# Fourteen of the first FFN's 22 inner tiles by seven block products instead of eight, with weight sums made by adding DMAs

## The chip, the cores and the metric

The kernel runs on one core of one Trainium2 chip. The metric is the device time of one execution in microseconds (us); lower is better. TensorE multiplies, VectorE, ScalarE and GpSimd work on tiles of 128 partitions in SBUF and PSUM, and SyncE (SP) issues most of the DMAs. In rows of the profile PE is TensorE, PEld its weight load, DVE VectorE, ACT ScalarE and POOL GpSimd.

## What is computed

The reference is a trunk of two layers on 512 tokens of width 1024: a conformer convolution module and an FFN, then retention with four heads and a second FFN. The change is in the first FFN (`F` = 2816, 22 tiles of 128 columns):

```python
def conv_ffn(x, w_in, dw_w, dw_b, w_out):
    h = x @ w_in                       # x (512, 1024), w_in (1024, 2 * 2816)
    a, u = jnp.split(h, 2, axis=-1)
    a = causal_dwconv(a, dw_w, dw_b)   # three taps along the tokens, each column by itself
    return (jax.nn.silu(a) * u) @ w_out

for i in range(DEPTH):
    ...
    h = rmsnorm(x, norm_ffn_g[i])
    x = x + conv_ffn(h, ffn_w_in[i], ffn_dw_w[i], ffn_dw_b[i], ffn_w_out[i])
```

Retention turns q and k by angles `positions * inv_freq`; the tables of their cosine and sine (128 x 512 each) are made while the first FFN runs.

## The kernel before

**Three matmuls for one.** Every operand is split into a high part that TensorE reads at its fast precision (type fp32r) and the low remainder, and a product is high x high, high x low and low x high, added up in PSUM (`mm3`, L272 to L274). Weights come from DRAM in chunks of up to 1 MB (`wr`, 128 x 2048), in the order in which they are used (`_chunks`), on SP's DMA queue. ScalarE casts a half of a chunk (128 x 1024) to its high part `wh` (L229) and VectorE subtracts it for the low part `wl` (L233). A unit of weights is what one call of `weights()` hands to TensorE, and the emission runs up to two units ahead of it; there are four buffers each for `wh` and `wl`.

**One inner tile of the FFN** (`ffn_half`, L785 to L831). `mm(f)` makes `fa` and `fu`, 128 inner columns x 512 tokens each, in PSUM: 8 row blocks x 3 matmuls with 512 columns moving. The x that they read is split before it is normalised, so each result still lacks the factor 1/rms of its token (`norm.rb`, shown as `n1r`). `evac(f)` puts it in: VectorE multiplies `fa` by it into `ap` (L812), ScalarE and VectorE do the three taps and SiLU (`ft`, L814 to L817), GpSimd scales `ft` for `fu`'s sake (L818), VectorE multiplies `fu` by it (`fy`, L820), and `fy` is split (`yh`, `yl`; L348, L349). After 12 tiles the output projection `fo0` multiplies their y's by `w_out` and adds to x, and after the other 10 `fo1` does. `fo1`'s additions also build the square sums for the next norm, n2.

**The tables.** `rotary_tables` (L836 to L877) is a generator: after each tile from the third on, one step of four GpSimd instructions on 128 x 512 is put out (multiply, round, subtract, add: L863, L856, L857, L871).

**Seven products.** Retention's value and gate projections already multiply 2 x 2 blocks with seven products in the heads 1 to 3 (`ret_vg_blocks`, tiles `vg1z` to `vg3p`). The sums of weight blocks for them are made by VectorE (L255), those of x by `left_sums` (L922 to L929).

A scheduler orders the instructions of each engine by an estimate of the time line; each engine then runs its own queue in that order and waits on semaphores.

## Time and profile before

| | us |
|---|---|
| median of 3 runs | 1292.96 |
| lowest, highest | 1292.64, 1293.29 |
| the profiled execution | 1293.24 |
| its span in the trace | 1291.5 |
| first FFN in it, by the rows of its tiles | about 182 to 549 |

TensorE's granted clock is at its full level (1.00) throughout the first FFN. Read the page from the share of each engine and the chain that ended last to the stage at hand; the busy times of the stage, not those of the span, tell what is free there.

### The profile page before, as it was taken

To read this page: it belongs to the slowest core of one execution; us is meant where nothing else is said; L and a number is where in the kernel's file an instruction comes from. 1 tells how busy PE (TensorE), PEld (TensorE's weight loads), DVE (VectorE), ACT (ScalarE), POOL (GpSimd) and SP (SyncE) were. 2 spreads that over 40 slices of the span, in tenths; PEclk is the share of its full clock that TensorE was granted. 3 is DMA by queue.
4 is the path that set the end of the run, shared out by engine and by line. 5 is a ranking of instruction groups with operands and counts; after the bars stand their busy time and mean duration, and the time that the engine had idled before them with its cause. 6 is when DMAs were issued, how large, how long until landed. Compare 5 with 4: busy or idle time off the path is not lost.

```text
span 1291.5 us, 15110 instructions
## 1 busy us (share of the span) xinstructions
PE 1282.0 (99%) x5955; PEld 1067.0 (83%) x5955; DVE 810.0 (63%) x1036; ACT 520.9 (40%) x703; POOL 355.2 (28%) x305
## 2 busy tenths in 40 slices
PE   9999999999999999999999999999999999999997
PEld 7889988888888888888888888878888888888886
DVE  6998657665335554579696596596675643355542
ACT  6646644333124333334435335354443431233332
...
GB/s 330 225 123 106 148 98 70 127 66 130 98 98 66 130 49 114 131 81 106 106 42 160 138 14 180 103 83 116 97 76 145 94 143 98 98 66 131 33 65 65
DMA packets 35926, 140.48 MB, mean 109 GB/s; under 512 B 10896, under 2 KB 15760, under 8 KB 21776
## 3 DMA queue, kind: packets, MB, share of 16 engines
q1 hardware_dynamic: 32256, 134.02, 30.2%
q10 hardware_dynamic: 3600, 5.52, 1.5%
q8 instruction: 46, 0.75, 0.2%
...
## 4 chain that ended last, share of the span: by engine, by line
PE 96%; DVE 2%; issue 1%; ACT 0%; POOL 0%; POOLq 0%
PE fa L272 6%; PE fa L274 6%; PE fu L273 6%; PE fu L272 6%; PE fu L274 6%; PE fa L273 6%; PE lo L272 3%; PE fo L273 3%; PE fo L274 3%; PE lo L273 3%; PE lo L274 3%; PE fo L272 3%; PE cph L539 2%; PE ro L272 2%; PE ro L273 2%; PE ro L274 2%
## 5 line engine op out<-in xcount | busy, mean ns | idle before, releaser
L233 DVE TENSOR_TENSOR wl<-wr,wh 128x1024 fp32r<-128x1024 f32 (+2 forms) x242 | 302.7, 1254 | 207.2 <-ACT wh L229 203.7
L229 ACT CAST wh<-wr 128x1024 fp32r<-128x1024 f32 (+2 forms) x244 | 250.5, 1029 | 372.0 <-PE fo L274 82.7
L811 POOL MEMSET ap<- 128x2 f32 x44 | 4.2, 99 | 371.7 <-DVE ft L816 305.4
L988 POOL TENSOR_TENSOR gg<-gg,gn 128x512 f32<-128x512 f32 x16 | 27.5, 1719 | 179.3 <-ACT gg L987 179.3
L820 DVE TENSOR_TENSOR fy<-fu,ft 128x512 f32<-128x512 f32 x44 | 30.4, 690 | 68.6 <-PE fu L274 35.0
L814 ACT ACTIVATE ft<-ap,prm 128x512 f32<-128x512 f32 x44 | 35.8, 814 | 71.3 <-DVE ap L812 71.3
L588 DVE SCALAR_TENSOR_TENSOR tp<-hp,prm,tp 128x512 f32<-128x512 f32 x80 | 55.8, 747 | 0.4
L579 POOL TENSOR_TENSOR pla<-pla,plt 128x512 f32<-128x512 f32 x36 | 49.1, 1365 | 9.8 <-ACT pla L575 5.7
L815 DVE SCALAR_TENSOR_TENSOR ft<-ap,prm,ft 128x512 f32<-128x512 f32 x44 | 37.2, 844 | 17.7 <-ACT ft L814 17.5
L817 ACT ACTIVATE ft<-ft 128x512 f32<-128x512 f32 x44 | 27.9, 633 | 45.0 <-DVE ft L816 44.6
L972 POOL TENSOR_TENSOR rs<-rs 128x512 f32<-128x512 f32 x16 | 24.7, 1559 | 67.5 <-DVE rs L971 43.7
L818 POOL TENSOR_TENSOR ft<-ft,n3r 128x512 f32<-128x512 f32 x22 | 32.1, 1461 | 29.0 <-ACT ft L817 29.0
L818 POOL TENSOR_TENSOR ft<-ft,n1r 128x512 f32<-128x512 f32 x22 | 31.6, 1434 | 28.8 <-ACT ft L817 28.8
L816 DVE SCALAR_TENSOR_TENSOR ft<-ap,prm,ft 128x512 f32<-128x512 f32 x44 | 35.8, 814 | 1.5
L578 ACT ACTIVATE plt<-hp,prm 128x512 f32<-128x512 f32 x36 | 25.8, 722 | 20.6 <-POOL pla L579 20.2
L539 PEld LDWEIGHTS cph<-ph,cmat 128*128 128x128 f32 x288 | 32.6, 192 | 0.2
L539 PE MATMUL cph<-ph,cmat 128*128 128x128 f32 x288 | 32.6, 275 | 0.0
L430 DVE TENSOR_TENSOR xT<-ro,xT 128x512 f32<-128x512 f32 x32 | 21.6, 682 | 15.6 <-PE ro L274 15.6
L255 DVE TENSOR_TENSOR wr<-wr,wr 128x1024 f32<-128x1024 f32 x24 | 28.8, 1211 | 0.0
L812 DVE TENSOR_TENSOR ap<-fa,n3r 128x512 f32<-128x512 f32 x22 | 15.1, 690 | 20.5 <-PE fa L274 20.5
L812 DVE TENSOR_TENSOR ap<-fa,n1r 128x512 f32<-128x512 f32 x22 | 15.1, 689 | 17.2 <-PE fa L274 17.2
L856 POOL TENSOR_SCALAR near<-prod 128x512 f32<-128x512 f32 x11 | 22.9, 2085 | 0.9
...
## 6 DMA issues: line engine op xcount, KB each, us to landing
wr<-in_weights_dram SPq DMA_DIRECT2D x106, 1024.0 KB, 4.9
...
wr<-in_weights_dram SPq DMA_DIRECT2D x4, 512.0 KB, 3.4
...
```

What stands on the lines that cost most here:

```text
L229: latest[0] = act.copy(hi[:, o:o + n], raw[:, s + o:s + o + n])
L233: latest[1] = low_on.get(i, dve).tensor_tensor(out=lo[:, o:o + n], in0=raw[:, s + o:s + o + n], in1=hi[:, o:o + n].bitcast(F32), op=ALU.su ...
L272: pe.matmul(ps, wh, xh, start=first, stop=False, **check)
L273: pe.matmul(ps, wl, xh, start=False, stop=False, **check)
L274: pe.matmul(ps, wh, xl, start=False, stop=last, **check)
L539: pe.matmul(ps[:, g * P:(g + 1) * P], mats[i][g][:, s, :], ph[:, g, NSH - 1 - s:NSH - 1 - s + P], start=s == 0, stop=s == NSH - 1)
L579: gate[0] = pool.tensor_tensor(out=pl, in0=pl, in1=tm, op=ALU.add).ins
L588: dve.scalar_tensor_tensor(out=a, in0=hp[:, t:t + S], scalar=tap(t, i), in1=a, op0=ALU.mult, op1=ALU.add)
L814: act.activation(t, ap[:, 2:], AF.Identity, scale=wc(2), bias=wc(3))
L815: dve.scalar_tensor_tensor(out=t, in0=ap[:, 1:1 + S], scalar=wc(1), in1=t, op0=ALU.mult, op1=ALU.add)
L816: dve.scalar_tensor_tensor(out=t, in0=ap[:, 0:S], scalar=wc(0), in1=t, op0=ALU.mult, op1=ALU.add)
L818: scaled = pool.tensor_tensor(out=t, in0=t, in1=norm.rb, op=ALU.mult)
```

## The change

Columns 8 to 13 and 14 to 21 of the 22 inner tiles are now made in pairs, a pair being 256 columns of a and the 256 of u that belong to them. Take x as 2 x 2 blocks (token half by half of the 1024 rows) and the pair's weights as 2 x 2 blocks (row half; a in column 1, u in column 2). Seven block products give the pair where eight did. Each product has 2 inner tiles x 4 row blocks x 3 matmuls with 256 columns moving. The groups of inner tiles are now 0 to 7 (as before), 8 to 13 and 14 to 21, each with its output projection (`fo0`, `fo1`, `fo2`).

- *Weights.* A pair's weights are two chunks `wr`, one holding W11 and W12, the next W21 and W22. The seven factors in order of use are W11, W21, `ws`, then W11, W12, W21, W22 again after sums have been added to them in place. `ws` = W11 + W12 is one VectorE addition into a buffer of its own. W12 += W22 is a DMA from DRAM that adds to what lies in SBUF; it is issued with the loads, during the pair before. W11 += W12 is an adding DMA within SBUF, issued when factor 1 is handed out, W21 += W11 the same at factor 2. All three are issued by GpSimd. Each factor is then cast and subtracted like any unit.
- *Left operands.* `Factors` makes four sums of the normalised x, one step per tile of the first group, and the normalised x itself is split anew ahead of `fo0`. The results of the second and third group therefore need no scaling by 1/rms, and GpSimd's L818 falls away for them.
- *Evacuation* (`ffn_blocks`). Five of the seven products run in one bank per tile, `fz`; between them ScalarE copies intermediate results out (`q1`, `u1`, `u2`). `fx` and `fp` are two more. The three taps (`taps`) are as before; the memset goes to VectorE.
- *Tables.* The same arithmetic on VectorE, a step per tile of the second and third group. Six tiles borrow buffers of other names (`rot0` to `rot5`).
- The pool of the FFN's tiles has 8 buffers for y where it had 12.

Core of the diff:

```diff
-HALVES = [(0, 12), (12, 22)]
+GROUPS = [[(0, 8, False), (8, 14, True), (14, 22, True)], [(0, 12, False), (12, 22, False)]]
...
     def ffn(l):
-        for f0, f1 in HALVES:
+        for f0, f1, by_blocks in GROUPS[l]:
             for f in range(f0, f1, 2):
-                cols("ffn_w_in", l, 0, 8, (f * P, 256))
-                cols("ffn_w_in", l, 0, 8, (F + f * P, 256))
...
+    def prepare_pair(i):
+        for j in (i, i + 1):
+            next(load_weights(j))
+        w = raws[i, "sum"] = sum_pool[0].tile([P, 1024], F32, tag="ws", bufs=1, name=f"ws{i}")
+        dve.tensor_tensor(out=w, in0=raws[i][:, :1024], in1=raws[i][:, 1024:], op=ALU.add)
+        pool.dma_start(raws[i][:, 1024:], weights_d[i + 1, :, 1024:], accum_op=ALU.add)
+    def pair_factor(i, n):
+        for j in (i, i + 2) if n == 3 else (i,):
+            if j in pairs and j not in raws:
+                prepare_pair(j)
+        w11, w12, w = raws[i][:, :1024], raws[i][:, 1024:], raws[i, "sum"]
+        w21, w22 = raws[i + 1][:, :1024], raws[i + 1][:, 1024:]
+        if n == 1:
+            pool.dma_start(w11, w12, accum_op=ALU.add)
+        if n == 2:
+            pool.dma_start(w21, w11, accum_op=ALU.add)
+        return (w11, w21, w, w11, w12, w21, w22)[n]
...
+        def turns(dst, src):
+            dve.tensor_scalar(out=near, in0=src, scalar1=MAGIC, scalar2=-MAGIC, op0=ALU.add, op1=ALU.add)
+            return dve.tensor_tensor(out=dst, in0=src, in1=near, op=ALU.subtract)
...
+    class Factors:
+        def __init__(self, norm, xs, pool_, other):
+            self.norm, self.xs, self.other = norm, xs, other
+            self.sums = [pool_.tile([P, 4, 4, N2], F32R, tag=f"s{half}", bufs=1, name=f"{norm.name}s{half}") for half in "hl"]
...
+        def sums_of(self, k):
+            x1, x2 = self.normed(k), self.normed(k + 4)
+            lo, hi = slice(0, N2), slice(N2, S)
+            a = xp.tile([P, 2, N2], F32, tag="nacc", bufs=1, name=f"{self.norm.name}sa{k}")
+            b = self.other(f"{self.norm.name}sb{k}")
+            dve.tensor_tensor(out=a[:, 0], in0=x1[:, hi], in1=x2[:, hi], op=ALU.subtract)
+            dve.tensor_tensor(out=a[:, 1], in0=a[:, 0], in1=x1[:, lo], op=ALU.subtract)
+            dve.tensor_tensor(out=b[:, 0], in0=x1[:, lo], in1=x1[:, hi], op=ALU.subtract)
+            dve.tensor_tensor(out=b[:, 1], in0=x2[:, lo], in1=a[:, 1], op=ALU.add)
+            for o, t in ((0, a), (2, b)):
+                h, l = (u[:, k, o:o + 2, :] for u in self.sums)
+                act.copy(h, t)
+                dve.tensor_tensor(out=l, in0=t, in1=h.bitcast(F32), op=ALU.subtract)
+        def normed_split(self, k):
+            self.xs[k] = split(self.normed(k), f"{self.norm.name}n{k}", ("xh", "xl"), xp8)
...
+    def ffn_blocks(fp, l, norm, f0, f1, left, side=None):
+        ys = []
+        for f in range(f0, f1, 2):
+            def bank(which):
+                return [psum(f"f{which}{l}_{f + j}")[:, :N2] for j in range(2)]
+            def product(pss, which, first=False):
+                w = weights()
+                for j, ps in enumerate(pss):
+                    for k, (xh, xl) in enumerate(left.factor(which)):
+                        mm3(ps, *w(k, j * P, (j + 1) * P), xh, xl, first and k == 0, k == 3, skip_group_check=not first)
+            def kept(pss, name):
+                tiles = [fp.tile([P, N2], F32, tag=name, bufs=2, name=f"{name}{l}_{f + j}") for j in range(2)]
+                for t, ps in zip(tiles, pss):
+                    act.copy(t, ps)
+                return tiles
+            lo, hi = slice(0, N2), slice(N2, S)
+            aps = [fp.tile([P, S + 32], F32, tag="ap", bufs=2, name=f"ap{l}_{f + j}") for j in range(2)]
+            us = [fp.tile([P, S], F32, tag="fy", bufs=2, name=f"fy{l}_{f + j}") for j in range(2)]
+            z = bank("z")
+            product(z, "x11", True)
+            q1 = kept(z, "q1")
+            x = bank("x")
+            product(x, "x12", True)
+            for j in range(2):
+                dve.memset(aps[j][:, :2], 0.0)
+                dve.tensor_tensor(out=aps[j][:, 2:2 + N2], in0=x[j], in1=q1[j], op=ALU.add)
+            p = bank("p")
+            product(p, "s1", True)
+            product(z, "s2")
+            u1 = kept(z, "u1")
+            product(z, "s3")
+            u2 = kept(z, "u2")
+            for j in range(2):
+                dve.tensor_tensor(out=us[j][:, hi], in0=p[j], in1=u2[j], op=ALU.subtract)
+            product(z, "x22")
+            ts = []
+            for j in range(2):
+                act.copy(aps[j][:, 2 + N2:2 + S], z[j])
+                ts.append(taps(fp, l, f + j, aps[j]))
+            product(p, "s4")
+            for j in range(2):
+                dve.tensor_tensor(out=us[j][:, lo], in0=p[j], in1=u1[j], op=ALU.subtract)
+                dve.tensor_tensor(out=us[j], in0=us[j], in1=ts[j], op=ALU.mult)
+                ys.append(split(us[j], f"y{l}_{f + j}", ("yh", "yl"), fp))
+                next(side or iter(()), None)
+        return ys
...
+        left = Factors(n1, list(n1.xs), fp, lambda name: fp.tile([P, 2, N2], F32, tag="fy", bufs=2, name=name))
+        def sums_of_x():
+            yield
+            for k in range(4):
+                left.sums_of(k)
                 yield
-    with ExitStack() as es:
-        fp = es.enter_context(tc.tile_pool(name="f0", reuse_waits="tile", bufs=12))
-        rp = es.enter_context(tc.tile_pool(name="rot", reuse_waits="tile", bufs=1))
-        n2 = Norm(mix_g[1], "n2")
-        rot = rotary_tables(rp)
-        for n, (f0, f1) in enumerate(HALVES):
-            ys = ffn_half(fp, 0, n1, f0, f1, () if n else (None, n1.stats, n1.bcast), rot)
-            proj_out(ys, f"fo{n}", n2 if n else None)
-        for _ in rot:
-            pass
+        for n, (f0, f1, by_blocks) in enumerate(GROUPS[0]):
+            if by_blocks:
+                ys = ffn_blocks(fp, 0, n1, f0, f1, left, rot)
+            else:
+                ys = ffn_half(fp, 0, n1, f0, f1, (None, n1.stats, n1.bcast), each=sums_of_x())
+                for k in range(KD):
+                    left.normed_split(k)
+                rot = rotary_tables(fp)
+                next(rot)
+            n2 = Norm(mix_g[1], "n2") if f1 == NF else None
+            proj_out(ys, f"fo{n}", n2)
+        assert next(rot, None) is None
```

On ScalarE, around tiles 16 and 17, stood before (`ft` the taps, `wh` a chunk's high part, `y0_16h` the high part of y):

```order
L814 ACTIVATE ft0_16_3582<-ap0_16_3579,prm_95 128x512
L817 ACTIVATE ft0_16_3582<-ft0_16_3582 128x512
L348 CAST y0_16h_3590<-fy0_16_3588 128x512
L229 CAST wh36_0_3456<-wr36_3454 128x1024
L229 CAST wh36_1024_3460<-wr36_3454 128x1024
L814 ACTIVATE ft0_17_3667<-ap0_17_3664,prm_95 128x512
L229 CAST wh37_0_3596<-wr37_3594 128x1024
L817 ACTIVATE ft0_17_3667<-ft0_17_3667 128x512
L229 CAST wh37_1024_3600<-wr37_3594 128x1024
```

and stands now (`q10_16`, `u10_16` copies of `fz`; `wh59` to `wh63` the high parts of factor 3 to 6 of one pair and 0 of the next, from `wr36` = W11, W12 and `wr37` = W21, W22):

```order
L239 CAST wh59_0_4128<-wr36_3856 128x1024
L929 COPY q10_16_4080<-fz0_16_4049 128x256
L929 COPY q10_17_4081<-fz0_17_4050 128x256
L239 CAST wh60_0_4156<-wr36_3856 128x1024
L385 CAST y0_14h_4027<-fy0_14_3782 128x512
L973 ACTIVATE ft0_15_3992<-ft0_15_3992 128x512
L239 CAST wh61_0_4188<-wr37_3858 128x1024
L239 CAST wh62_0_4222<-wr37_3858 128x1024
L929 COPY u10_16_4184<-fz0_16_4049 128x256
L385 CAST y0_15h_4037<-fy0_15_3783 128x512
L929 COPY u10_17_4185<-fz0_17_4050 128x256
L239 CAST wh63_0_4262<-wr38_4121 128x1024
```

The casts of `wh59` to `wh61` read weights to which an adding DMA has written; the copies `u10_16` and `u10_17` now stand behind `wh61`, whose sum is the last of the three to be issued.

On GpSimd stood before, in the first half (here at tile 4), a table step and the scaling of each tile:

```order
L818 TENSOR_TENSOR ft0_4_2273<-ft0_4_2273,n1r_1923 128x512
L863 TENSOR_SCALAR prod_2130<-rc0_2122 128x512
L856 TENSOR_SCALAR near_2131<-prod_2130 128x512
L857 TENSOR_TENSOR prod_2130<-prod_2130,near_2131 128x512
L871 TENSOR_TENSOR turn_2129<-turn_2129,prod_2130 128x512
L811 MEMSET ap0_7_2519 128x2
```

and in the second and third group stand now only the adding DMAs, three to a pair (here those into `wr36`, `wr37` and into `wr38`, `wr39`):

```order
L282 DMA wr36_3856<-in_weights_dram 128x1024
L292 DMA wr36_3856<-wr36_3856 128x1024
L294 DMA wr37_3858<-wr36_3856 128x1024
L282 DMA wr38_4121<-in_weights_dram 128x1024
L292 DMA wr38_4121<-wr38_4121 128x1024
L294 DMA wr39_4123<-wr38_4121 128x1024
```

On VectorE stood before, for tile 17 (`ap` the evacuation, L815 and L816 the taps, `wl` low parts):

```order
L812 TENSOR_TENSOR ap0_17_3664<-fa0_17_3529,n1r_1923 128x512
L233 TENSOR_TENSOR wl36_1024_3461<-wr36_3454,wh36_1024_3460 128x1024
L815 SCALAR_TENSOR_TENSOR ft0_17_3667<-ap0_17_3664,prm_95,ft0_17_3667 128x512
L816 SCALAR_TENSOR_TENSOR ft0_17_3667<-ap0_17_3664,prm_95,ft0_17_3667 128x512
L233 TENSOR_TENSOR wl37_0_3597<-wr37_3594,wh37_0_3596 128x1024
L820 TENSOR_TENSOR fy0_17_3673<-fu0_17_3554,ft0_17_3667 128x512
L233 TENSOR_TENSOR wl37_1024_3601<-wr37_3594,wh37_1024_3600 128x1024
L349 TENSOR_TENSOR y0_17l_3676<-fy0_17_3673,y0_17h_3675 128x512
```

and stands now, where the pair of 14 and 15 ends and that of 16 and 17 runs (L503 and L490 are a table step's, `ws38` the next pair's sum):

```order
L281 TENSOR_TENSOR ws38_4125<-wr38_4121 128x1024
L972 SCALAR_TENSOR_TENSOR ft0_15_3992<-ap0_15_3781,prm_95,ft0_15_3992 128x512
L243 TENSOR_TENSOR wl59_0_4129<-wr36_3856,wh59_0_4128 128x1024
L942 TENSOR_TENSOR ap0_16_4045<-fx0_16_4084,q10_16_4080 128x256
L243 TENSOR_TENSOR wl60_0_4157<-wr36_3856,wh60_0_4156 128x1024
L386 TENSOR_TENSOR y0_14l_4028<-fy0_14_3782,y0_14h_4027 128x512
L503 TENSOR_SCALAR rot0_2532<-rot4_2536 128x512
L941 MEMSET ap0_17_4046 128x2
L942 TENSOR_TENSOR ap0_17_4046<-fx0_17_4085,q10_17_4081 128x256
L959 TENSOR_TENSOR fy0_15_3783<-fy0_15_3783,ft0_15_3992 128x512
L243 TENSOR_TENSOR wl61_0_4189<-wr37_3858,wh61_0_4188 128x1024
L490 TENSOR_SCALAR rot1_2533<-rot0_2532 128x512
```

Low parts come closer together, and the evacuations are of 256 columns.

## Rows read from the trace of the kernel before

**Rows 1.** The page: busy time by engine, and the last chain by engine.

```profile
PE 1282.0 (99%) x5955; PEld 1067.0 (83%) x5955; DVE 810.0 (63%) x1036; ACT 520.9 (40%) x703; POOL 355.2 (28%) x305
...
PE 96%; DVE 2%; issue 1%; ACT 0%; POOL 0%; POOLq 0%
```

**Rows 2.** Busy time by stretch: tiles 0-11, `fo0`, tiles 12-21, `fo1`.

```profile
core 0: us, PE busy (x) PEld busy (x) DVE busy (x) ACT busy (x) POOL busy (x), PEclk, DMA share, GB/s
182.00:314.00 132.00, 132.00 (x584) 108.94 (x583) 85.94 (x93) 51.36 (x65) 79.47 (x62) 1.00 0.27 89
314.00:358.00 44.00, 44.00 (x195) 36.42 (x195) 13.91 (x15) 9.46 (x11) 7.69 (x5) 1.00 0.33 116
358.00:505.00 147.00, 147.00 (x650) 121.72 (x649) 72.60 (x82) 49.88 (x59) 30.48 (x27) 1.00 0.27 93
505.00:549.00 44.00, 43.68 (x193) 35.52 (x191) 24.84 (x25) 17.78 (x24) 9.06 (x6) 1.00 0.36 121
sum 367.00, PE 366.68 PEld 302.61 DVE 197.29 ACT 128.47 POOL 126.69; mean PE 91.67 PEld 75.65 DVE 49.32 ACT 32.12 POOL 31.67
```

**Rows 3.** Time line of TensorE (start, duration in us): one tile's `fa`.

```profile
303.39 0.39 PE L272 MATMUL fa<-n1x0h,wh 128*128 128x512 f32 x1
303.62 0.39 PE L273 MATMUL fa<-n1x0h,wl 128*128 128x512 f32 x1
...
308.83 0.39 PE L272 MATMUL fu<-n1x0h,wh 128*128 128x512 f32 x1
```

**Rows 4.** Time line of TensorE: 256 columns in scores and convolution output.

```profile
138.16 0.64 PE L281 MATMUL co<-z1h,wl 128*128 128x256 f32 x4
138.64 0.64 PE L283 MATMUL co<-z1l,wh 128*128 128x256 f32 x4
...
666.95 0.28 PE L273 MATMUL sc<-qk100h,qk110l 128*128 128x256 f32 x1
667.07 0.28 PE L274 MATMUL sc<-qk100l,qk110h 128*128 128x256 f32 x1
667.19 0.28 PE L272 MATMUL sc<-qk101h,qk111h 128*128 128x256 f32 x1
```

**Rows 5.** Time line of VectorE from 440 us; in brackets idle before, and releaser.

```profile
440.73 1.23 DVE L233 TENSOR_TENSOR wl<-wr,wh 128x1024 fp32r<-128x1024 f32 x1 [0.45 <-ACT wh L229]
441.87 0.75 DVE L815 SCALAR_TENSOR_TENSOR ft<-ap,prm,ft 128x512 f32<-128x512 f32 x1
442.65 0.75 DVE L816 SCALAR_TENSOR_TENSOR ft<-ap,prm,ft 128x512 f32<-128x512 f32 x1
...
445.85 0.69 DVE L820 TENSOR_TENSOR fy<-fu,ft 128x512 f32<-128x512 f32 x1 [1.18 <-POOL ft L818]
446.46 1.22 DVE L233 TENSOR_TENSOR wl<-wr,wh 128x1024 fp32r<-128x1024 f32 x1
...
455.98 0.69 DVE L820 TENSOR_TENSOR fy<-fu,ft 128x512 f32<-128x512 f32 x1 [2.34 <-PE fu L274]
```

**Rows 6.** VectorE by line: count, busy us, mean ns, idle before.

```profile
L812 DVE TENSOR_TENSOR ap<-fa,n1r 128x512 f32<-128x512 f32 x22 | 15.1, 689 | 17.2 <-PE fa L274 17.2
L922 DVE TENSOR_TENSOR sa<-xn,xn 128x256 f32<-128x256 f32 x4 | 1.7, 415 | 0.0
```

**Rows 7.** Instructions of line 846 (ns: lowest, median, highest).

```profile
L846 DVE TENSOR_SCALAR rc<-ang x1: 420/420/420, 221.5 to 221.5; 128x512 int32<-128x512 int32 x1
```

**Rows 8.** ScalarE: by line, and two starts of its time line.

```profile
L229 ACT CAST wh<-wr 128x1024 fp32r<-128x1024 f32 x234 | 245.5, 1051 | 369.7 <-PE fo L274 82.7 <-PE fa L274 77.7 <-PE lo L273 71.0
L814 ACT ACTIVATE ft<-ap,prm 128x512 f32<-128x512 f32 x44 | 35.8, 814 | 71.3 <-DVE ap L812 71.3
L817 ACT ACTIVATE ft<-ft 128x512 f32<-128x512 f32 x44 | 27.9, 633 | 45.0 <-DVE ft L816 44.6
L348 ACT CAST y_16h<-fy 128x512 fp32r<-128x512 f32 x2 | 1.2, 621 | 4.8 <-DVE fy L820 4.8
L1030 ACT COPY q<-vg1z 128x512 f32<-128x512 f32 x2 | 1.2, 588 | 1.8 <-PE vg1z L274 1.8
...
439.64 1.05 ACT L229 CAST wh<-wr 128x1024 fp32r<-128x1024 f32 x1 [1.68 <-PE fa L274]
440.60 0.81 ACT L814 ACTIVATE ft<-ap,prm 128x512 f32<-128x512 f32 x1
```

**Rows 9.** GpSimd by line.

```profile
L856 POOL TENSOR_SCALAR near<-prod 128x512 f32<-128x512 f32 x11 | 22.9, 2085 | 0.9
L871 POOL TENSOR_TENSOR turn<-turn,prod 128x512 f32<-128x512 f32 x9 | 15.2, 1694 | 0.5
L863 POOL TENSOR_SCALAR prod<-rc 128x512 f32<-128x512 f32 x10 | 15.1, 1507 | 0.6
L857 POOL TENSOR_TENSOR prod<-prod,near 128x512 f32<-128x512 f32 x10 | 14.4, 1440 | 0.8
L811 POOL MEMSET ap<- 128x2 f32 x44 | 4.2, 99 | 371.7 <-DVE ft L816 305.4 <-ACT wh L229 48.2 <-ACT ft L814 17.9
```

**Rows 10.** DMA issues: count, KB each, median us from issue to landing.

```profile
wr<-in_weights_dram SPq DMA_DIRECT2D x106, 1024.0 KB, 4.9
wr<-in_weights_dram SPq DMA_DIRECT2D x4, 512.0 KB, 3.4
xT<-in_xt_dram SPq DMA_DIRECT2D x2, 512.0 KB, 7.7
```

**Rows 11.** Waits of TensorE's loads: us in total, times, longest; `vg1` has none.

```profile
PEld vg3p L274 <- DVE wl L233: 1.4, 2, 0.9
PEld vg3z L274 <- DVE wl L233: 1.0, 1, 1.0
PEld vg3z L272 <- ACT wh L229: 0.5, 1, 0.5
```

More of the change, by code (lines that the diff above doesn't have):

```diff
@@ L75, in _chunks, with cols @@
 def _chunks():
-    out, blocks = [], []
-    def cols(w, l, r0, nk, *ranges):
-        out.append((w, l, r0, nk, ranges))
+    out, blocks, pairs = [], [], []
+    def cols(w, l, r0, nk, *ranges, apart=False):
+        out.append((w, l, r0, nk, ranges, apart))
     for c in range(2):
@@ L128, in _chunks @@
     ffn(1)
-    return out, blocks
+    return out, blocks, pairs
 LINE = 256
@@ L211, in split_raw @@
     def split_raw(raw, i, unit, ends=None):
-        nk, ncol = descs[i]
+        nk, ncol = descs[i] if i not in pairs else (4, 256)
         per = 1024 // ncol
@@ L242, in emit_weights @@
         i, n = units[unit]
+        if i in pairs:
+            for _ in split_raw(pair_factor(i, n), i, unit):
+                pass
+            return
         if n is None:
@@ L782, in trunk, with normed, factor @@
         proj_out(zs, "co", n1, between=lambda k: run(SEQ_OUT.get(k, "")))
-    def ffn_half(fp, l, norm, f0, f1, hooks=(), side=None):
+    N2 = S // 2
+    class Factors:
+        def __init__(self, norm, xs, pool_, other):
+            self.norm, self.xs, self.other = norm, xs, other
+            self.sums = [pool_.tile([P, 4, 4, N2], F32R, tag=f"s{half}", bufs=1, name=f"{norm.name}s{half}") for half in "hl"]
+        def normed(self, k):
+            n = self.norm
+            t = xp.tile([P, S], F32, tag="nsq", bufs=2, name=f"{n.name}n{k}")
+            dve.scalar_tensor_tensor(out=t, in0=xT[k], scalar=n.gain[:, k:k + 1], in1=n.rb, op0=ALU.mult, op1=ALU.mult)
+            return t
+        def sums_of(self, k):
[13 more added lines that the diff above has]
+            self.xs[k] = split(self.normed(k), f"{self.norm.name}n{k}", ("xh", "xl"), xp8)
+        def factor(self, which):
+            if which[0] == "s":
+                j = int(which[1]) - 1
+                return [tuple(u[:, k, j, :] for u in self.sums) for k in range(4)]
+            t = slice(0, N2) if which[1] == "1" else slice(N2, S)
+            return [tuple(u[:, t] for u in self.xs[k + (4 if which[2] == "2" else 0)]) for k in range(4)]
@@ new lines, in taps, with wc @@
+    def taps(fp, l, f, ap):
+        def wc(j):
+            return fw[l][:, j * NF + f:j * NF + f + 1]
+        t = fp.tile([P, S], F32, tag="ft", bufs=3, name=f"ft{l}_{f}")
+        act.activation(t, ap[:, 2:2 + S], AF.Identity, scale=wc(2), bias=wc(3))
+        dve.scalar_tensor_tensor(out=t, in0=ap[:, 1:1 + S], scalar=wc(1), in1=t, op0=ALU.mult, op1=ALU.add)
+        dve.scalar_tensor_tensor(out=t, in0=ap[:, 0:S], scalar=wc(0), in1=t, op0=ALU.mult, op1=ALU.add)
+        act.activation(t, t, AF.Silu)
+        return t
@@ L786, in ffn_half @@
+    def ffn_half(fp, l, norm, f0, f1, hooks=(), side=None, each=None):
         ys, wt, mid = [], {}, {}
@@ L1023, in product @@
                 for tb in range(2):
-                    for k, (xh, xl) in enumerate(left(which)):
+                    for k, (xh, xl) in enumerate(left.factor(which)):
                         t = slice(tb * P, (tb + 1) * P)
@@ L1142, in trunk @@
         for k in range(KD):
-            normed_split(k)
+            left.normed_split(k)
         for h in range(1, H):
```

154 lines of the change are left out of this document (67 added, 87 removed).

## The prediction

> **What bounds the kernel now.** I read the page from its first part down, then the stage that the change touches. TensorE is busy for 1282.0 of 1291.5 us, and the chain that ended last is 96% TensorE [rows 1]: time is gained only by giving TensorE less to stream, or lost by making it wait. The change lies in the first FFN, 182 to 549 us. There TensorE is idle for 0.3 of 367 us at full clock, VectorE is busy for 197, ScalarE for 128 and GpSimd for 127 [rows 2]. So today the feeding engines have about half their time free here, and the question is what is left of that when the weights' sums and splits are added.
>
> The unit of account is a pair of inner tiles (256 columns of a, 256 of u).
>
> **TensorE's term.** Before, a pair is 2 tiles x 2 parts x 8 row blocks x 3 = 96 matmuls of 512 columns. Twenty-four of them, from 303.39 to 308.83 us, take 5.44 us, so 0.2267 us each [rows 3], and a pair 21.76 us. After, a pair is 7 products x 2 tiles x 4 row blocks x 3 = 168 matmuls of 256 columns. No row shows this FFN with 256 columns, but two other stages stream 256 columns with a new stationary operand each time: 0.12 us from start to start in the scores, and 0.48 us for four in the convolution's output [rows 4]. So a product is 24 x 0.12 = 2.88 us, a pair 20.16 us, and a pair saves 1.60 us, not the eighth (2.72 us) that the column count promises, because two matmuls of 256 columns take 0.24 us where one of 512 takes 0.2267. Seven pairs: **11.2 us**. The output projections keep their 528 matmuls; cutting them into three groups instead of two changes only where they stand.
>
> A rule of the Trainium skill prices this otherwise: TensorE: Matmul & The Clock Gate, section Back-to-back issue gap, gives 262 cycles for 256 columns and 518 for 512 at 2.4 GHz, an estimate of 109 and 216 ns. By it a pair would fall from 20.7 to 18.3 us and seven pairs would save 16.9 us; the rows have 120 and 227 ns, and I go by them.
>
> **VectorE's load.** Its instructions overlap, so I price them from start to start: a 128x1024 subtraction 1.14 us, a scalar-tensor-tensor over 512 0.78, a tensor-tensor over 512 0.61 [rows 5]. A 256-wide one has a mean of 0.415 us where a 512-wide one has 0.69 [rows 6]; with the same overlap of 0.08 it costs 0.335. A tensor-scalar over 512 in SBUF lasted 0.42 us [rows 7], so 0.34. A pair after: 7 low parts and 1 sum (9.12), six 256-wide evacuations (2.01), four taps (3.12), two products and two low parts of y (2.44), two short memsets (0.2, by GpSimd's 0.10 each [rows 9]): 16.9 us. Each step of the rotary table is two tensor-scalars and two tensor-tensors, 1.9 us, about two steps to a pair: 3.8. Sum 20.7 us against TensorE's 20.16 if both steps fall inside; counted along the new order, the busiest pair holds 19.8. VectorE goes from half used to full in these pairs. It isn't yet the bound, since it may run up to three products ahead (four buffers of high and low parts), and in each output projection it recovers: in today's first one, its additions included, it is busy for 13.9 of 44 us [rows 2], and the normed splits put 8 x (0.78 + 0.61) = 11.1 us on that.
>
> **ScalarE**: seven casts of 0.96 from start to start, eight 256-wide copies of at most 0.59 (the row for 512 out of PSUM), and 2 x (0.81 + 0.63 + 0.62) = 4.1 for taps, SiLU and y [rows 8]: at most 15.5 of 20.16 us. **Group of the first eight tiles**: VectorE had 86 of 132 us for 12 tiles, so some 57 of 87 for eight; the left sums add 4 x 4.1 = 16.5. That fits. GpSimd loses the table's steps (four to a term, 1.4 to 2.1 us each) and the scaling of these 14 tiles [rows 9]; nothing on the chain waited for them, so this gains nothing by itself, except that VectorE's two-input instructions no longer share with them.
>
> **The new waits.** (a) One bank z takes five products of the seven. Between product 4 and 5, and 5 and 6, ScalarE has to copy z out while TensorE runs the other tile's half, 1.44 us. A copy of at most 0.59 behind one cast of 1.05 needs 1.64 in the worst meeting; usually it just fits. (b) The added factors. GpSimd issues W11 += W12 after factor 1 is split and W21 += W11 after that, SBUF to SBUF, and ScalarE's cast of the sixth factor waits for both. Behind that cast in ScalarE's queue stand the copies of product 4, for which TensorE's product 5 waits. The chain: the previous pair's product 4 ends and frees a weight buffer, cast 1.05, low part 1.22 with two evacuations ahead 0.67, add, add, two casts 2.1, copy 0.4 (between 0.59 and a third of it), some 0.6 for signals; then product 5 may start. That is 6.0 us plus two adds in the 7 x 2.88 = 20.16 us between the one product 4 and the next: each add may take **7.1 us** from issue to landing before TensorE waits.
>
> No row shows an adding DMA or a DMA of GpSimd's. Below stands the plain 512 KB load, 3.4 us; above, the 512 KB load that shared the engines at the start, 7.7; the 1024 KB load, 4.9 us, moves as many bytes as an add has to read [rows 10]. I take 5 to 6, near the 4.9 with GpSimd's issue, and so a hidden chain with some 2 to 4 us to spare. The DRAM add (W12 += W22) is issued a pair earlier and has 20 us. SP's next loads now wait for the adds that read their buffers; each lands 4.9 us after issue and VectorE has over 9 us of other work before it needs one.
>
> The nearest rows for what remains of such waits are those of the retention stage, which uses the same seven products in three heads: TensorE's loads waited 1.4 + 1.0 + 0.5 = 2.9 us for weights in all, all of it in the third head, none in the other two [rows 11]. A mean of 1.0 a head is 7 us for seven pairs, the best two heads give 0. I take 1.7, a quarter microsecond a pair, since the products are half as long as there and nearly everything else is hidden. After the second group the last y comes late (its low part stands behind a weight split on VectorE), but the scheduler put eight matmuls of the next chunk ahead, so nothing more is added.
>
> **Sum against the profiled execution**: 1293.24 - 11.2 + 1.7 = 1283.7 us. That execution is 0.28 above the median of the runs, so the forecast is **1283.5 us**; with waits between 0 and 5 us, 1281.4 to 1287.
>
> **Rivals.** *The adds are slower than 7.1 us* (ends slower). Place: ScalarE's cast of the sixth factor in the five pairs that follow another pair. Price: two adds a pair, so 10 us of the kernel for each microsecond over 7.1; from 8.1 us on the gain is gone. For it: each add reads twice what a 512 KB load reads, and is issued by GpSimd, whose full-width rows take 1.4 to 2.1 us [rows 9]: 2 x 3.4 + 2.1 = 8.9 gives 1283.5 + 18 = 1301.5 us. Against: a second 512 KB in one load adds only 1.5 us [rows 10]. A rule of the Trainium skill stands on its side: SBUF — State Buffer, section Who interferes with whom, says that GpSimd's writing of descriptors is shut out while VectorE runs a two-port instruction, as the table's tensor-scalars would be. No run here shows it; four of 0.42 us a pair would put at most 1.7 us on the two adds together. Chance 0.17.
>
> *VectorE becomes the bound*: if it waits 2 us a pair for inputs that come just in time, its busiest pairs take some 22 us; the five pairs with table steps lose 1.9 each less the lead that two projections give back (3 us): 6.5 us over the forecast, 1290. Idle gaps of 1 to 2.4 us before fy and wl in the rows of today speak for it [rows 5]; that such gaps vanish when the queue is full speaks against. Chance 0.16.
>
> *256 columns stream in other time here*: at half of a 512's 0.2267 us [rows 3] a pair saves the full eighth, 2.72, and the time is 1275.6, chance 0.03 (the page TensorE: Matmul & The Clock Gate of the Trainium skill stands on that side). Or the load of the stationary operand sets the pace, 1067.0 us for 5955 loads [rows 1], 0.18 each: 168 x 0.18 = 30.2 us a pair, 59 us more in seven, 1352 us, which [rows 4] exclude but for 0.01. The change does what it says: the new program holds 168 matmuls a pair.
>
> **Chances.** Forecast (1281.4 to 1287) 0.63; VectorE bound (1287 to 1293) 0.16; adds slow (1290 to 1310) 0.17; the full eighth 0.03; the load's pace 0.01. A measurement of this kernel tells about 0.2%, 2.6 us, from no change. Faster than 1290.4: 0.63 + 0.03 + 0.09 of VectorE's case; within: 0.07 + 0.03 of the adds'; slower 0.14 + 0.01. The range 1281 to 1295 leaves out the full eighth, the load's pace and the slower part of the adds, some 0.17.
>
> **What would show it.** A product of 2.88 us and seven to 20.2 us in TensorE's rows of fz, fx, fp; landing times of GpSimd's DMAs below 7 us; VectorE busy above 90% in the pairs and TensorE's waits in them below 2 us together; nothing moved after 549 us but the start. I am wrong if ScalarE's casts wait for DMA with TensorE idle behind them, or if TensorE's waits sit on VectorE's low parts.

## The result, and the profile after

The changed kernel takes **1281.4 us** (median of 4 runs, 1281.16 to 1281.55), the kernel before 1293.12 beside it. The ratio is 0.9909, with a 95% interval of 0.9892 to 0.9926: 11.7 us faster. The forecast was 1283.5 us, in a range of 1281 to 1295. The profiled execution took 1281.37 us, its span 1279.6.

The page of the changed kernel, answering to [rows 1] and [rows 10] (busy time by engine, the chain that ended last, and DMA issues with their median time from issue to landing):

```profile
PE 1270.1 (99%) x6459; PEld 1082.6 (85%) x6459; DVE 882.9 (69%) x1210; ACT 566.1 (44%) x796; POOL 271.0 (21%) x250
...
PE 97%; DVE 2%; issue 1%; POOL 0%; ACT 0%; POOLq 0%
...
wr<-in_weights_dram SPq DMA_DIRECT2D x106, 1024.0 KB, 5.0
...
wr<-wr POOLq DMA_DIRECT2D x14, 512.0 KB, 4.5
wr<-in_weights_dram POOLq DMA_DIRECT2D x7, 512.0 KB, 5.9
```

TensorE is still the bound, with 504 instructions more and 11.9 us less of busy time. The last two rows are the adding DMAs, 14 within SBUF and 7 from DRAM.

TensorE's time line at the start of products (start and duration in us), where [rows 3] and [rows 4] stood before:

```profile
313.94 0.28 PE L309 MATMUL fz<-n1n0h,wh 128*128 128x256 f32 x1
...
316.81 0.28 PE L309 MATMUL fx<-n1n4h,wh 128*128 128x256 f32 x1
316.93 0.28 PE L310 MATMUL fx<-n1n4h,wl 128*128 128x256 f32 x1
...
319.69 0.28 PE L309 MATMUL fp<-n1sh,wh 128*128 128x256 f32 x1
...
336.97 0.28 PE L309 MATMUL fx<-n1n4h,wh 128*128 128x256 f32 x1
```

A product takes 316.81 to 319.69, 2.88 us; from one pair's second product to the next one's, 316.81 to 336.97, are 20.16 us. The view of TensorE's waits lists none for another engine or a DMA between 182 and 545 us.

Busy time by stretch, each from one pair's second product to the next one's where the next pair follows (same columns as [rows 2]; the stretches of 20.40 and 20.55 us hold two and three matmuls of the next pair besides):

```profile
316.81:336.97 20.16, 20.16 (x170) 20.16 (x169) 13.05 (x19) 11.86 (x18) 2.60 (x3) 1.00 0.68 177
336.97:357.37 20.40, 20.40 (x172) 20.40 (x171) 19.60 (x32) 12.95 (x20) 2.60 (x3) 1.00 0.62 153
430.12:450.28 20.16, 20.16 (x170) 20.16 (x169) 19.45 (x30) 11.92 (x19) 1.74 (x2) 1.00 0.63 165
450.28:470.83 20.55, 20.55 (x173) 20.55 (x172) 19.35 (x31) 14.41 (x24) 3.46 (x4) 1.00 0.71 180
```

VectorE (third pair of figures) is busy for 19.4 to 19.6 us of a pair with table steps, ScalarE for 11.9 to 14.4, and TensorE for all of it at full clock. In the first pair of each group, without table steps, VectorE has much time left (13.1 us in the first row).

**Where the 11.9 us of span went.** From the first matmul of `fa` to the first of the queries, the first FFN took 182.33 to 542.75 us before, 360.42, and 182.00 to 531.33 after, 349.33: 11.09 less. It began 0.33 earlier. From the first query matmul to the first value matmul it took 23.92 us before and 23.12 after, 0.80 less: a wait of TensorE's loads there, of 0.7 us for a low part of x, is gone:

```profile
PEld qk L274 <- DVE n2x6l L352: 0.7, 1, 0.7
```

What follows is 0.3 longer.

### The profile page after: what moved, and what is told of

Its sections match the earlier page's. It is cut to its first block, busy times and chain, and to the rows that moved or that the text cites. A ratio compares the mean times of both kernels' runs of the same rounds, so it can differ in the third digit from the quotient of the medians.

```text
span 1279.6 us, 16389 instructions
## 1 busy us (share of the span) xinstructions
PE 1270.1 (99%) x6459; PEld 1082.6 (85%) x6459; DVE 882.9 (69%) x1210; ACT 566.1 (44%) x796; POOL 271.0 (21%) x250
## 4 chain that ended last, share of the span: by engine, by line
PE 97%; DVE 2%; issue 1%; POOL 0%; ACT 0%; POOLq 0%
PE fu L310 4%; PE fa L310 4%; PE fa L311 4%; PE fu L311 4%; PE fa L309 4%; PE fu L309 4%; PE fo L310 3%; PE fo L309 3%; PE fo L311 3%; PE lo L310 3%; PE lo L311 3%; PE lo L309 3%; PE cph L622 3%; PE qk L309 2%; PE qk L310 2%; PE qk L311 2%
## 5 line engine op out<-in xcount | busy, mean ns | idle before, releaser
L243 DVE TENSOR_TENSOR wl<-wr,wh 128x1024 fp32r<-128x1024 f32 (+2 forms) x256 | 314.9, 1234 | 164.4 <-ACT wh L239 161.8
L239 ACT CAST wh<-wr 128x1024 fp32r<-128x1024 f32 (+2 forms) x258 | 264.9, 1030 | 329.2 <-PE lo L310 63.5
L1003 DVE TENSOR_TENSOR fy<-fu,ft 128x512 f32<-128x512 f32 x30 | 20.6, 688 | 39.3 <-PE fu L311 23.9
L971 DVE SCALAR_TENSOR_TENSOR ft<-ap,prm,ft 128x512 f32<-128x512 f32 x44 | 33.9, 771 | 11.6 <-ACT ft L970 11.4
L972 DVE SCALAR_TENSOR_TENSOR ft<-ap,prm,ft 128x512 f32<-128x512 f32 x44 | 33.9, 771 | 0.8
L311 PE MATMUL fp<-n1sl,wh 128*128 128x256 f32 x112 | 31.7, 283 | 0.0
L310 PE MATMUL fp<-n1sh,wl 128*128 128x256 f32 x112 | 31.7, 283 | 0.0
L309 PE MATMUL fp<-n1sh,wh 128*128 128x256 f32 x112 | 31.7, 283 | 0.0
L311 PE MATMUL fz<-n1sl,wh 128*128 128x256 f32 x112 | 31.6, 283 | 0.0
L310 PE MATMUL fz<-n1sh,wl 128*128 128x256 f32 x112 | 31.6, 283 | 0.0
## 6 DMA issues: line engine op xcount, KB each, us to landing
cmat<-in_mats_dram SPq DMA_DIRECT2D x4, 2304.0 KB, 11.2
```

Source lines behind the costliest of these rows:

```text
L239: latest[0] = act.copy(hi[:, o:o + n], raw[:, s + o:s + o + n])
L243: latest[1] = low_on.get(i, dve).tensor_tensor(out=lo[:, o:o + n], in0=raw[:, s + o:s + o + n], in1=hi[:, o:o + n].bitcast(F32), op=ALU.su ...
L309: pe.matmul(ps, wh, xh, start=first, stop=False, **check)
L310: pe.matmul(ps, wl, xh, start=False, stop=False, **check)
L311: pe.matmul(ps, wh, xl, start=False, stop=last, **check)
L971: dve.scalar_tensor_tensor(out=t, in0=ap[:, 1:1 + S], scalar=wc(1), in1=t, op0=ALU.mult, op1=ALU.add)
```

## The experiments

Theory: the gain is TensorE's stream, 1.60 us a pair, and all that feeds it is hidden. The rivals are those of the prediction. Each run is set against runs of the kernel before beside it (1293.5 to 1293.7; the changed kernel stood 11.7 below its own).

| kernel | median us | less than before beside it |
|---|---|---|
| changed kernel | 1281.4 | 11.7 |
| e1, eight pairs | 1280.4 | 13.3 |
| e2, four pairs | 1286.7 | 7.1 |
| e3, four adds in a chain | 1320.9 | -27.1 |
| e4, sums by VectorE | 1281.65 | 12.1 |
| e5, three adds in a chain | 1291.2 | 2.3 |
| e6, tables by GpSimd | 1289.0 | 4.5 |
| e7, both FFNs | 1296.8 | -3.4 |
| e8, sums and more by VectorE | 1301.3 | -7.8 |
| e9, both FFNs, own staging tile | 1286.0 | 7.5 |
| e10, plain tiles with 256 columns | 1287.5 | 6.0 |
| e11, tables by GpSimd, sums by VectorE | 1288.5 | 4.9 |
| e12, both FFNs, ten plain tiles | 1322.1 | -28.6 |

### What a pair is worth: e1 and e2

```diff
-[(0, 8, False), (8, 14, True), (14, 22, True)]
+[(0, 6, False), (6, 14, True), (14, 22, True)]      # e1
+[(0, 8, False), (8, 14, False), (14, 22, True)]     # e2, x split anew and six table steps put out after the second group
```

> One more pair by seven products: the plain group is tiles 0 to 5 instead of 0 to 7, the groups of pairs are 6 to 13 and 14 to 21. Theory (TensorE's stream is the whole gain, a pair is 21.76 us before and 20.16 after, nothing waits): 1.60 us less than the 1281.4 of the changed kernel, 1279.8, within 0.5. Rival (VectorE becomes the bound in the first group, where the same left sums, 16.5 us, now meet 6 tiles' work in 65 us, and the normed splits follow at once): the gain is gone, 1281 to 1285, with TensorE's first pair waiting for the left sums or for the low parts of x.

> Tiles 8 to 13 go back to eight products (plain tiles, scaled by GpSimd as in the first group), 14 to 21 stay with seven: four pairs instead of seven. Theory (each pair is worth 1.60 us of stream, and nothing else of the change is worth anything): 1281.4 + 3 x 1.60 = 1286.2, within 0.7. Rival (part of the gain comes from what the change took from GpSimd or from a place outside the pairs): the time isn't linear in the number of pairs, below 1284 or above 1288.

In e2 the last eight tiles read an x to which the first projection has already been added, so its numbers are not those wanted; the work is the same. Four, seven and eight pairs gain 7.1, 11.7 and 13.3 us: 1.57 us a pair between the ends, and 0.8 us that doesn't depend on their number, which is the size of the wait that left the queries (from the first query to the first value matmul both kernels take 23.1 us, as the changed one does). In both kernels the view of TensorE's waits lists none for another engine in the FFN. So the gain is linear in the pairs, as the theory has it. In e1 VectorE was busy for 52.9 of the first 66 us, and the left sums were in time. e1 beats both kernels, by 1.6 us over the changed one; in its trace the first FFN takes 347.71 us against 349.33.

### Why 1.6 and not 2.7: e10

```diff
-for k in range(KD):
-    mm3(ps, *wt[which](k, o, o + P), *norm.xs[k], k == 0, k == KD - 1)
+for t in (first 256 tokens, last 256 tokens):       # first FFN's plain tiles
+    for k in range(KD):
+        mm3(ps[:, t], *wt[which](k, o, o + P), *(u[:, t] for u in norm.xs[k]), k == 0, k == KD - 1)
```

> The first eight tiles keep their eight products, but each matmul of 512 columns is made as two of 256 (first the 256 earlier tokens of all row blocks, then the later ones), 768 matmuls instead of 384; nothing else changes. Theory (two matmuls of 256 take 0.240 us where one of 512 takes 0.2267, which is why a pair gave 1.60 us and not 2.72): 384 x 0.0133 = 5.1 us more, 1281.4 + 5.1 = 1286.5. Rival (the pace depends on the columns alone and the missing eighth was lost elsewhere): 1281.4.

5.7 us were lost (11.7 to 6.0) where 5.1 were forecast, 5.55 of them in the trace between the first `fa` and `fo` (88.42 to 93.97 us). The time line shows the same operands at the pace of [rows 4]:

```profile
205.17 0.28 PE L309 MATMUL fu<-n1x2h,wh 128*128 128x256 f32 x1
205.29 0.28 PE L310 MATMUL fu<-n1x2h,wl 128*128 128x256 f32 x1
205.41 0.28 PE L311 MATMUL fu<-n1x2l,wh 128*128 128x256 f32 x1
```

The missing part of the eighth is the price of narrower matmuls: 0.120 us each, not 0.113. The 262 cycles that the Trainium skill gives for 256 columns, for a single matmul by itself (TensorE: Matmul & The Clock Gate, Back-to-back issue gap), an estimate of 109 ns at 2.4 GHz, aren't reached here. The rows are 120 ns apart. Each matmul has a new stationary operand; whether that is the reason wasn't tested.

### How long an add may take: e3 and e5

```diff
     if n == 1:
         pool.dma_start(w11, w12, accum_op=ALU.add)
+        pool.dma_start(w11, w12, accum_op=ALU.add)   # e3 and e5
     if n == 2:
         pool.dma_start(w21, w11, accum_op=ALU.add)
+        pool.dma_start(w21, w11, accum_op=ALU.add)   # e3 only
```

> Both adding DMAs within SBUF are issued twice, one behind the other, so that a pair's chain holds four of them instead of two (the second time the same block is added once more, so the sums are not those wanted). They landed in 4.5 us each in the changed kernel. Theory of the prediction (a chain of 6.0 us and the adds has to fit into 20.16 us, so the adds together may take 14.1): 4 x 4.5 = 18.0, 3.9 us too much in each of five pairs that follow another pair: 1281.4 + 19.5 = 1301, with TensorE waiting in front of the sixth product. Rival (the chain was drawn too long, its casts and copies have more slack than I counted): less than 1 us a pair, below 1287.

> Only the first of the two adding DMAs within SBUF is issued twice, so a chain holds three of them (the same block is added twice, so the sums are not those wanted). Theory of the prediction (the adds together may take 14.1 us): one behind the other they were issued 4.9 to 5.2 us apart in the kernel with four, so three take about 15.2, which is 1.1 us a pair too much in five pairs: 1281.4 + 5.5 = 1287, if so short a wait leaves the clock alone. Rival (with four, which took 20.6 us, TensorE waited for 23.3 us in five places, 4.7 each, so the limit lies near 15.9): three are still hidden, below 1282.5.

GpSimd's time line in e3 (start, duration; L292, L293, L295 and L296 are the four adds, one behind the other):

```profile
440.56 0.86 POOL L292 DMA_DIRECT2D wr<-wr  x1 [11.82 <-DVE fy L952]
445.50 0.89 POOL L293 DMA_DIRECT2D wr<-wr  x1 [4.08 <-DMA wr<-wr]
450.66 0.87 POOL L295 DMA_DIRECT2D wr<-wr  x1 [4.27 <-DVE ws L281]
451.30 1.12 POOL L282 DMA_DIRECT2D wr<-in_weights_dram  x1
455.87 0.86 POOL L296 DMA_DIRECT2D wr<-wr  x1 [3.44 <-DMA wr<-wr]
```

The waits of TensorE (us in total, times, longest), of e3 and then of e5, whose weight loads are listed:

```profile
PE fz L311 <- ACT u L931: 22.3, 5, 8.4
PE fo L311 <- ACT wh L239: 4.8, 1, 4.8
```

```profile
PEld fz L310 <- ACT u L930: 5.8, 5, 2.0
```

In the chain shown the adds follow each other at 4.9 to 5.2 us, so three take some 15.2. With three, TensorE waited 5.8 us in five places, at the place that the prediction named: product 5, for the copies that ScalarE has queued behind the sixth factor's cast (the expectation of e3 says in front of the sixth product, which is wrong). The mean of 1.2 off 15.2 gives 14.0, where the prediction had 14.1. So near a match holds for the mean alone: by TensorE's starts and the landings of the adds, the single waits are 0.2 to 2.0 us, the three adds take 14.6 to 16.9 from the first issue to the last landing, and each pair by itself gives 12.8 to 15.7. That three adds are still hidden, the rival limit of 15.9, falls.

The time rose by more than the waits: by 7.9 us in the profiled execution, and to 1289.3 to 1293.4 over ten runs. In the profiled one the clock fell behind one of the waits, that of 1.8 us which ended at 464.0 (granted clock third from the end):

```profile
463.00:466.00 3.00, 2.00 (x15) 2.00 (x16) 3.00 (x5) 2.94 (x6) 0.00 (x0) 0.92 0.92 356
466.00:469.00 3.00, 3.00 (x16) 3.00 (x16) 2.23 (x5) 0.81 (x3) 0.86 (x1) 0.51 0.77 259
```

Why the ten runs spread as they do isn't shown, as only one of them has a trace. In e3 the clock did more: the kernel lost 38.8 us with 27.6 of waiting. Its stretches of 3 us around one wait:

```profile
349.00:352.00 3.00, 0.00 (x0) 0.00 (x0) 0.98 (x2) 0.00 (x0) 1.01 (x1) 1.00 1.03 201
352.00:355.00 3.00, 0.00 (x0) 0.00 (x0) 0.00 (x0) 0.36 (x1) 0.00 (x0) 0.60 0.49 96
355.00:358.00 3.00, 1.05 (x5) 1.05 (x6) 2.28 (x3) 3.00 (x6) 0.00 (x0) 0.50 0.75 243
358.00:361.00 3.00, 3.00 (x16) 3.00 (x16) 3.00 (x5) 1.01 (x2) 0.00 (x0) 0.50 0.68 236
361.00:364.00 3.00, 3.00 (x20) 3.00 (x20) 1.01 (x4) 1.32 (x2) 0.88 (x1) 0.70 0.66 150
364.00:367.00 3.00, 3.00 (x27) 3.00 (x26) 2.41 (x3) 2.39 (x4) 0.87 (x1) 1.00 0.37 70
```

After TensorE stood idle from about 349 to 357 us, the clock granted was 0.50 (1.2 GHz), and when it started again it passed 16 matmuls in 3 us where it passes 27 at 1.00. So the waits of e3 were paid nearly one and a half times, which its expectation (1301) left out; the waits too were longer than the 19.5 us forecast.

### Whether VectorE bounds: e4 and e8

```diff
-pool.dma_start(w11, w12, accum_op=ALU.add)                # likewise W21 += W11 and W12 += W22
+dve.tensor_tensor(out=w11, in0=w11, in1=w12, op=ALU.add)
+# e8 besides: the low parts of factors 3, 4 and 5 are computed twice
```

> The three adding DMAs of a pair become three VectorE additions of 128x1024 in the same place. By the prediction's prices VectorE then has 16.9 + 3.8 + 3.4 = 24.1 us of work in a pair of 20.16. Theory (VectorE was full but not the bound, and with 3.4 us more it becomes it): in the pairs with table steps TensorE waits for low parts, some 2 to 3 us a pair after a lead of about 8 us a group is used up, 1281.4 + 6 to 14 = 1287 to 1295. Rival (VectorE's order has so much slack that TensorE never sees it): 1281 to 1283.

> The weight sums by VectorE as before, and three of the seven low parts of a pair computed twice, so VectorE gets 3 x 1.14 = 3.4 us more in a pair. With the sums alone it was busy for 20.16 of 20.16 us in the later pairs and TensorE never waited, what was late being done in the projection behind. Theory (it is full and lives on its lead): now it becomes the bound, 2 to 3.4 us a pair in the four or five pairs that follow another one, 1281.6 + 8 to 17, and more if TensorE's clock falls after a wait. Rival (work that isn't needed at once, y's low parts and table steps, gives way further): below 1285.

Stretches of a pair in e4, and then the waits of TensorE in e8:

```profile
337.51:357.70 20.19, 20.19 (x171) 20.19 (x170) 20.19 (x29) 12.99 (x21) 0.00 (x0) 1.00 0.23 80
430.69:450.85 20.16, 20.16 (x171) 20.16 (x170) 20.14 (x28) 12.96 (x21) 0.00 (x0) 1.00 0.32 106
```

```profile
PE fz L311 <- DVE wl L244: 8.3, 4, 5.6
PE fz L311 <- DVE ap L942: 5.0, 2, 3.2
```

e4 fell outside the theory's range: VectorE was busy for every microsecond of the pairs, and TensorE didn't wait for any of it (12.1 us below before, against 11.7). Full is not late. What isn't needed at once (the low parts of y, table steps) is done in the projection that follows, where VectorE was busy for 37.1 of 41.3 us, 4.4 more than in the changed kernel:

```profile
369.19:410.53 41.34, 41.34 (x219) 35.67 (x218) 37.06 (x56) 14.90 (x20) 0.00 (x0) 1.00 0.30 103
```

Another 3.4 us a pair was too much: in e8 TensorE waited 13.3 us for VectorE, one wait was followed by a clock of 0.81 in its stretch of 10 us, and the time rose by 19.9 over e4. So the adding DMAs save nothing by themselves: three VectorE additions in their place give the same time.

### Where the tables belong: e6 and e11

```diff
-dve.tensor_scalar(out=near, ...); dve.tensor_tensor(out=dst, ...)     # all steps of the tables
+pool.tensor_scalar(out=near, ...); pool.tensor_tensor(out=dst, ...)   # e6; e11 has e4's sums as well
```

> The table steps go back to GpSimd in their new places (the two masking instructions stay with VectorE), everything else as changed. GpSimd then has two steps of four instructions, 13.4 us, in a pair, and in its order one or two table instructions of 1.4 to 2.1 us stand between the first and the second adding DMA. Theory (two adds of 4.5 and up to 3.6 between them are 12.6 to 13.5, less than 14.1, and VectorE's relief is worth nothing as it didn't bound): no change, 1281 to 1283. Rival A (adds queued behind table steps come late): 1 to 3 us a pair in the five or six pairs with steps, above 1286. Rival B (VectorE's relief is worth something): below 1280.8.

> Tables on GpSimd and weight sums on VectorE: GpSimd issues no adding DMA any more. With the tables on GpSimd and the adding DMAs kept, the time was 1289.0. Theory (what cost there were the adds that came late behind table steps): gone here, 1281 to 1283. Rival (GpSimd's table steps and VectorE's two-input instructions slow each other, taps 900 ns there against 771 in the changed kernel, so VectorE bounds): VectorE has the sums' 3.4 us a pair on top and the loss stays or grows, 1286 or above.

e6 lost 7.3 us, e11 6.8, so both theories missed. Late adds can't be the whole cause, as e11 has none. Both have long VectorE instructions. Time line of e6, VectorE first, then GpSimd:

```profile
411.06 2.83 DVE L243 TENSOR_TENSOR wl<-wr,wh 128x1024 fp32r<-128x1024 f32 x1 [0.39 <-ACT wh L239]
...
431.48 2.33 DVE L971 SCALAR_TENSOR_TENSOR ft<-ap,prm,ft 128x512 f32<-128x512 f32 x1
```

```profile
411.17 1.63 POOL L491 TENSOR_TENSOR rot<-rot,rot 128x512 f32<-128x512 f32 x1
...
431.63 1.62 POOL L491 TENSOR_TENSOR rot<-rot,rot 128x512 f32<-128x512 f32 x1
```

The low part that starts 0.11 us ahead of a GpSimd tensor-tensor lasts 2.83 us where the median is 1.22, and the tap 2.33 where it is 0.75: each is longer by 1.6 us, the length of the GpSimd row. The longest low part of the pairs is 1226 ns in the changed kernel, 3144 in e6 and 2312 in e11 (instructions of the line, in ns):

```profile
L243 DVE TENSOR_TENSOR wl<-wr,wh x49: 1209/1218/1226, 315.6 to 487.3; 128x1024 fp32r<-128x1024 f32 x49
```

```profile
L243 DVE TENSOR_TENSOR wl<-wr,wh x47: 1206/1226/3144, 315.6 to 487.4; 128x1024 fp32r<-128x1024 f32 x47
```

The Trainium skill (SBUF — State Buffer, Who interferes with whom) says that a VectorE instruction with two SBUF inputs contends with a GpSimd instruction that reads SBUF, and that the one that comes second is shut out for the whole instruction; these lengths agree with a block of that size. By the records VectorE's two instructions began first, by 0.11 and 0.15 us, so their order here doesn't tell which is shut out.

In e6 the adds were later too: one pair's first add was issued at 425.83 us, right behind a table instruction (423.53, 2.35 us long). But TensorE didn't wait for that. Its long waits in e6, all in front of product 5, and what led to the second of them:

```profile
PE fz L309 <- ACT u L929: 5.1, 3, 2.2
```

```profile
440.74 1.41 POOL L491 TENSOR_TENSOR rot<-rot,rot 128x512 f32<-128x512 f32 x1
...
441.27 1.43 DVE L959 TENSOR_TENSOR fy<-fy,ft 128x512 f32<-128x512 f32 x1
...
442.73 0.62 ACT L385 CAST y_15h<-fy 128x512 fp32r<-128x512 f32 x1 [2.46 <-DVE fy L959]
443.26 0.64 ACT L929 COPY u<-fz 128x256 f32<-128x256 f32 x2
...
443.68 0.39 PE L309 MATMUL fz<-n1sh,wh 128*128 128x256 f32 x1 [1.87 <-ACT u L929]
```

ScalarE's copy stands in its queue behind the cast of a y, and that cast waited for VectorE's `fy` (0.68 us long in the changed kernel, 1.43 here), in all three places: 2.53, 2.46 and 1.11 us. The casts that read the adds' sums were done before. Only in front of the first of the three does the chain, followed further back, run through an adding DMA. In e11 TensorE waited in the same way, for copies behind a y, for low parts, and in a projection for a y itself. So what cost the time was chiefly VectorE, late by what GpSimd did beside it; rival A named the size for e6, not the cause.

### Both FFNs: e7, e9 and e12

```diff
-[(0, 12, False), (12, 22, False)]                                          # second FFN
+[(0, 6, False), (6, 10, True), (10, 16, True), (16, 22, True)]             # e7, e9
+[(0, 6, False), (6, 10, False), (10, 16, True), (16, 22, True)]            # e12
-xq = lp.tile([P, 4, NTB, kn, QB], F32, tag="xq", ...)                      # staging of x by tokens
+xq = fp.tile([P, 4, NTB, kn, QB], F32, tag="ws", ...)                      # e7: two blocks at a time
+xq = xp.tile([P, 4, NTB, 1, QB], F32, tag="rbc", ...)                      # e9: one; e12: three such tiles in turn
```

> Seven products in both FFNs: 6 plain tiles and 8 pairs in the first, 6 plain tiles and 8 pairs in the second (groups of 6, 4, 6 and 6 tiles, six buffers for y, the token-major copy of x staged in the sum's buffer). Theory (a pair is worth 1.60 us of TensorE's stream wherever its feeding fits): 1281.4 - 1.6 - 8 x 1.6 = 1267.0, plus up to 2 us for the last projection, whose last y come closer to its start. Rival (the second FFN lacks room: two buffers for taps, transposes beside the left sums, so that low parts come late): 1 us or more a pair is lost, 1275 or above.

> As the kernel with seven products in both FFNs, but the token-major copy of x is staged in a tile of its own (one block at a time) and no longer in the buffer of the pairs' sums. In that one TensorE waited for 15.9 us at the third product of the second FFN's first pair, for the cast of a sum whose buffer was still held by that staging, and the pairs after it took 20.16 us each. Theory (that buffer was all that was wrong): 1281.4 - 1.6 - 12.8 = 1267.0, plus up to 2 for the last projection: 1267 to 1270. Rival (128 small transfers on SP's queue stand in front of weight loads and hold them): a wait of 5 us or more at the first pair, 1273 or above.

> Seven products in both FFNs once more: 6 plain tiles and 8 pairs in the first, 10 plain tiles (groups of 6 and 4) and 6 pairs in the second, the left sums of x spread over both plain groups, the token-major copy through three staging tiles and in the first plain group only. In the two earlier kernels of this kind VectorE was full in the second FFN's first 6 tiles, and TensorE stood still at the first pair for want of the staging tile. Theory (feeding fits now, a pair is worth 1.60 us there too): 1281.4 - 1.6 - 6 x 1.6 = 1270.2, plus up to 2 for the last projection: 1270 to 1272.5. Rival (the staging still comes too late): 1275 or above, with TensorE waiting behind the additions of the second FFN's first projection.

All three missed. The pairs themselves ran as forecast, here two of e7 in the second FFN, 20.16 us apart:

```profile
1104.18 0.28 PE L309 MATMUL fx<-n3n4h,wh 128*128 128x256 f32 x1
...
1124.34 0.28 PE L309 MATMUL fx<-n3n4h,wh 128*128 128x256 f32 x1
```

What was lost stands around the first two projections there, one longest wait in each (TensorE in e7 and e9, ScalarE in e12):

```profile
PE fp L309 <- ACT wh L239: 15.7, 1, 15.7
```

```profile
PE lo L309 <- DVE xt L1295: 6.7, 1, 6.7
```

```profile
ACT wh L239 <- DMA wr<-in_weights_dram: 57.8, 2, 56.1
```

In e7 a sum's buffer waited for the staging, in e9 the projections' additions waited for it, and in e12 weight loads on SP's queue stood behind 128 small transfers, which SP issued without a load between them from 952 to 1036 us, 16 in some 10.3. ScalarE waited 56.1 us for a load there. An estimate from TensorE's starts: without what the second FFN lost by waits and by the clock behind them (29.0, 17.2 and 51.6 us more than in the changed kernel) the three would take about 1268, 1268 and 1272 us, as forecast. So the second FFN could be worth as much, but a staging of x that fits beside it was not found; no kernel here shows the gain.

## Why the prediction was right, point by point

**TensorE's term** held: 2.88 us a product, 20.16 a pair, 11.2 forecast and 11.09 measured in the FFN; e1 and e2 give 1.57 a pair. The estimate that the prediction set beside it by the Trainium skill (TensorE: Matmul & The Clock Gate, Back-to-back issue gap) comes to 16.7 us for seven pairs, not 16.9; the trace doesn't bear it out.

**The waits** were the term that was off. 1.7 us was taken from the heads of [rows 11]; measured was 0.0. Those were waits for weights, low parts above all, and in the FFN none came late. The other wait that the prediction weighed, a copy behind a cast, didn't come either: ScalarE's 256-wide copy took 0.37 us and not up to 0.59, so one behind a cast of 1.05 needs 1.42 of the 1.44 that TensorE gives it. The two in the changed kernel:

```profile
346.08 1.05 ACT L239 CAST wh<-wr 128x1024 fp32r<-128x1024 f32 x1
347.25 0.37 ACT L929 COPY u<-fz 128x256 f32<-128x256 f32 x1
```

Without waits the prediction's own sum is 1293.24 - 0.28 - 11.2 = 1281.8; the 1281.4 that it has as the lower end of its range is 0.4 too low. That the median is 1281.4 to the decimal is luck: the 0.8 us at the queries, which no step foresaw, took it there. What removed the wait at the queries wasn't tested.

**VectorE's load** was priced well: 19.8 us forecast for the busiest pair, 19.4 to 19.6 measured. The rival supposed that VectorE's idle gaps of some 2 us a pair stay when its queue is full. They don't: in e4 it was busy for 20.14 to 20.19 us of a pair, and TensorE had no wait. e8 shows that a wait begins within the next 3.4 us.

**The adds**: 5 to 6 us were taken, 4.5 measured. Two of the 14 within SBUF took longer than the limit of 7.1 for one (7.3 and 7.9), without a wait, as each had a fast one behind it: the one of 7.9 and the next together took 13.3 us from issue to landing, and the limit of 14.1 is on both. It lies within what e5's pairs give (12.8 to 15.7, mean 14.0), and the place of the wait was right. The one add issued while a table's tensor-scalar ran on VectorE, at 470.02 us, landed in 4.5 as well. The rival's price, 10 us of the kernel for each microsecond over the limit of 7.1 an add, was too low, since it left out the clock: by it e5 would have lost 5.5 us, and it lost 9.4.

**GpSimd's relief** was costed at nothing, apart from VectorE's rows no longer sharing with it. That clause was worth more than its words: with the tables left on GpSimd 7 of the 11.7 us are gone (e6, e11). The prediction would have missed a version of the change without it.

**A pair early**: what it is worth to issue the next pair's loads, its `ws` and its DRAM add during the pair before was not run; no run here shows it.
